# Rows on all partitions from columns: transposes of a broadcast column in place of products with a fixed matrix

## Chip, cores and metric

The kernel runs as one program on one core of a Trainium2 chip. The metric is the time of one execution in device microseconds (us). The engines are called as in the profile: PE (TensorE, matrix products), PEld (its weight loads), DVE (VectorE), ACT (ScalarE), POOL (GpSimd), and SP, whose queue issues the DMAs.

## What is computed

The reference takes 256 tokens of width 1024 in f32 through two networks, one behind the other. The first has two layers, each with a feed-forward block, a mixer and a second feed-forward block; the mixer is a hybrid (a state-space scan, "SSD", beside an mLSTM) in layer 0 and a sparse attention in layer 1. The second has two layers, each with three branches (gated MLP, retention, gated delta rule), gates and an output product. The parts that the change touches, cut short:

```python
# feed-forward block, before: x + 0.5 * swiglu(rms_norm(x))
y = xf * rsqrt(mean(xf * xf) + EPS) * g
# hybrid, SSD: decays between the tokens t and s of one chunk of 128
acs = cumsum(dt * A)
Lm = exp(where(t >= s, acs[t] - acs[s], -inf))
# hybrid, mLSTM: stabilised weights
Dm = where(t >= s, bcs[t] - bcs[s] + li[s], -inf)
m_t = maximum(max(Dm, axis=s), bcs + m_in)
S = (q @ k.T) * exp(Dm - m_t)
# delta rule, per direction, chunks of 64
gc = cumsum(g)
decay = exp(where(i >= j, gc[i] - gc[j], -inf))
lower = where(i > j, ((k * b) @ k.T) * decay, 0)
u, w = solve_triangular(lower + eye, rhs)
```

All four need the same thing at one point: a value per token, which lies in a column (token t on partition t), is wanted as a row that every partition holds (element t of the row belongs to token t), so that differences such as `acs[t] - acs[s]` can be formed on a 128 x 128 tile.

## The kernel before, in words

**Tiling.** The tokens are two tiles of 128. Each weight matrix comes from memory once, in units of 128 x 2048 f32, by DMAs from SP's queue (L273; three buffers). Every unit is split in halves of 1024 columns. ACT makes a rounded copy `hi` of a half (L218), DVE the rest `lo` = raw - `hi` in two instructions of 512 columns (L222), and there are four buffers each for `hi` and `lo`. An f32 product of the weights is then three products of this split form (L306 to L308, `mm3`): hi*hi, hi*lo and lo*hi. Activations are turned for these products by transposes against the identity matrix (`flip`, L478).

**Small products in plain f32.** Beside these large products there are small ones in plain f32, among them the ones that the change touches. They use a fixed trick: with a column v broadcast along the free dimension as the stationary operand, and a fixed matrix M as the moving one, the product holds on every partition the row v^T M. With M the identity (`ident`) this is the row of v itself; with M the triangular matrix `tri` (ones where the column index is at least the row index; `rtri` for the reverse direction) it is the running sum of v as a row.

**The four places.**

- Feed-forward block (`ffn`, L499; four calls). `rstd[t]`, the reciprocal root of a token's mean square, is spread to a row by two products with `ident` (L519), copied by ACT, and used from the second group of columns on, to scale the gate.
- Hybrid, decays (`decays`, L722; called for two groups of 8 heads). One product with `tri` sums all columns `a` to running sums (L668), which L670 copies to `cs`. Per group, chunk and head the product at L730 makes the running sum as a row once more, out of `a` and `tri`: 2 x 2 x 8 = 32 products into four-head tiles of PSUM. L733 on DVE subtracts the column `cs` and cuts off with `cap`; exponentials and products follow.
- Hybrid, mLSTM. Running maxima are formed on 4 partitions (one per head) as rows `R`; L811 negates two of them (`nR`, 4 x 256); four transposes (L814) turn `R` into columns `pw`; L816 and the exponentials make weights `w` from them. Behind a turn of side work, L828 spreads the rows of `nR` over all partitions: four products, each of a column of `ident[:4]` broadcast to 4 x 128 with `nR`, 256 columns. L832 on DVE takes them up.
- Delta rule (`delta`, L1293; once in each of the second network's two layers). Four products sum the columns `gs` to running sums (L1356 to L1359), which L1361 copies to `gc` on DVE. Then for two directions, two tiles and four heads L1368 makes the running sums as rows out of `gs` and `tri` or `rtri`: 16 products. L1372 on DVE and L1375 and L1376 on ACT make the decays `D`; products of keys with keys (L1390) and L1394 and L1398 on DVE fill the triangular system `U`, and L1405 adds the two directions. From there DMAs (L1424, L1428) carry it to the layout in which POOL solves 32 x 32 blocks (L1430 to L1436), and DMAs bring it back (L1443 to L1446). Later the blocks are put together; this stage begins with L1487 and the transposes at L1412.

**What sets the order.** In the hybrid and in the second network two generators are woven: a chain of dependent small steps, and side work (large weight products of other branches). The tables FILL (L602) and SIDE (L1245) say how many steps of side work follow each step of the chain. On top of this the instructions' order on each engine is set by the framework's planner when the program is built: it simulates all engines with durations of its own and takes the next ready instruction by priority, which is the order of writing. In sections marked `manual` (the sparse attention, the start and the ends of the down products) the written order stays. None of the four places lies in such a section.

Of the kernel before, what the change touches and what calls it, by code (L numbers as in the profile page):

```python
# [13 lines left out]
OP = mybir.AluOpType  # L14
# [32 lines left out]
class Entry:  # L47
# [17 lines left out]
    def load(self, dram, between=None):  # L65
        self.raw.append(self.net.fetch(dram, 2048, between))
# [53 lines left out]
class Net:  # L120
# [43 lines left out]
    def dram(self, shape):  # L164
        self.n += 1
        return self.dp.tile(shape, F32, name=f"dram{self.n}")

    def load_const(self, name, cols, parts=128):
        t = self.const(cols, parts=parts)
        self.nc.sync.dma_start(t, self.ins[name])  # L170
        return t
# [327 lines left out]
    def ffn(self, f, then):  # L499

        nc = self.nc
        V, A, PE = nc.vector, nc.scalar, nc.tensor
        hT, rstd, ps = self.entry.hT, self.entry.rstd, self.entry.out
        hid = Wide(self.f, 0)

        hid.grow(self.f)
        p = self.pt().rearrange("p (t j c) -> p t j c", j=2, t=2)
        for t in range(2):
            sg, hd = self.t2(256), self.t2(256)
            A.activation(sg, ps[t][:, :256], AF.Silu, scale=rstd[t])  # L510
            V.tensor_tensor(hd, ps[t][:, 256:], sg, OP.mult)
            for j in range(2):
                PE.transpose(p[:, t, j, :], hd[:, j * 128:(j + 1) * 128], self.ident)
        parts = lambda j: (a[:, :, j % 4:j % 4 + 2, :] for a in hid.half[-1])
        self.split(*parts(0), p)

        pr = self.pt()
        for t in range(2):
            PE.matmul(pr[:, t * 128:(t + 1) * 128], rstd[t].to_broadcast([128, 128]), self.ident, start=True, stop=True)  # L519
        row = self.l2(256)  # L520
        A.activation(row, pr[:, :256], AF.Copy)
        half = [self.small(1) for _ in range(2)]
        for t in range(2):
            nc.gpsimd.tensor_scalar(half[t], rstd[t], 0.5, None, op0=OP.mult)

        for j in range(2, 2 * NFG):
            if j % 4 == 0:
                hid.grow(self.f if j < 16 else self.g)
            if j % 2 == 0:
                hd = self.t2().rearrange("p (t j c) -> p t j c", t=2, j=2)  # L530
            gate, up = (x[:, :256] for x in self.group_w(self.ins["wgw"][f, j - 2], hT))
            sg = self.t2(256)
            V.tensor_tensor(sg, gate, row, OP.mult)
            A.activation(sg, sg, AF.Silu)
            tc = lambda z: z.rearrange("p (t c) -> p t c", t=2)
            V.tensor_tensor(hd[:, :, j % 2, :], tc(up), tc(sg), OP.mult)
            if j % 2:
                self.split(*parts(j - 1), hd)

        def done(t, cb, p):  # L540
            s = self.x[t][:, cb * 512:(cb + 1) * 512]
            V.scalar_tensor_tensor(s, p, half[t], s, op0=OP.mult, op1=OP.add)  # L542

        self.down(self.ins["wdn"][f], 2 * NFG, hid.tok, done, then)
# [60 lines left out]
class Hybrid:  # L605
    def hybrid(self, then):
        nc = self.nc
        ins = self.ins
        V, A, PE, G = nc.vector, nc.scalar, nc.tensor, nc.gpsimd
        mm = PE.matmul  # L610
# [36 lines left out]
        def chain():  # L647
# [16 lines left out]
            a = self.small(40).rearrange("p (t c) -> p t c", t=2)  # L664
# [4 lines left out]
            cs = self.small(40).rearrange("p (t c) -> p t c", t=2)  # L669
# [52 lines left out]
            def decays(g):  # L722

                for c in range(2):
                    seg[c] = self.g().rearrange("p (e t) -> p e t", e=8)
                    for hb in range(2):
                        pr = self.pt().rearrange("p (e t) -> p e t", e=4)
                        for e in range(4):
                            h = g * 8 + hb * 4 + e
                            mm(pr[:, e, :], a[:, c, h:h + 1].to_broadcast([128, 128]), self.tri, start=True, stop=True)  # L730
                        for e in range(4):
                            h = g * 8 + hb * 4 + e
                            V.scalar_tensor_tensor(seg[c][:, hb * 4 + e, :], pr[:, e, :], cs[:, c, h:h + 1], self.cap,  # L733
                                                   op0=OP.subtract, op1=OP.min)
                for c in range(2):
                    for hb in range(2):
                        half = seg[c][:, hb * 4:hb * 4 + 4]
                        A.activation(half, half, AF.Exp)
                        V.tensor_tensor(half, half, cb[:, c, g, None, :].to_broadcast([128, 4, 128]), OP.mult)
# [39 lines left out]
            A.activation(bt, pb[:, :256].rearrange("p (g n) -> p g n", g=2), AF.Copy)  # L779
            states(0)  # L780
            decays(0)
            yield next(fill)
            inputs(1)
            outputs(0)
            yield next(fill)
            turn(0)
            states(1)
            decays(1)
            yield next(fill)
            outputs(1)  # L790
# [10 lines left out]
            R = self.t2()  # L801
# [5 lines left out]
            V.tensor_tensor_scan(r4[:, 1], u4[:, 1], u4[:, 1], m1[:4], OP.max, OP.max)  # L807
            V.tensor_scalar(r4[:, 2], r4[:, 1], -1.0, m1[:4], op0=OP.mult, op1=OP.add)
            V.tensor_scalar(r4[:, 3], u4[:, 0], r4[:, 0, 127:128], None, op0=OP.subtract)
            nR = self.t2(256)  # L810
            V.tensor_scalar(nR[:4], R[:4, :256], -1.0, None, op0=OP.mult)  # L811
            pw = self.pt()
            for k in range(4):
                PE.transpose(pw[:, k * 4:k * 4 + 4], r4[:, k], self.ident[:4, :4])  # L814
# [2 lines left out]
                            pw[:, :8].rearrange("p (t c) -> p t c", t=2), OP.add)  # L817
            A.activation(w[:, :8], w[:, :8], AF.Exp, scale=-1.0)
            A.activation(w[:, 8:], pw[:, 8:16], AF.Exp)
            em = w[:, :8].rearrange("p (t c) -> p t c", t=2)  # L820
            yield next(fill)
            turn(1)
# [2 lines left out]
            for hb in range(2):  # L825
                pr = self.pt().rearrange("p (h c s) -> p h c s", h=2, c=2)
                for h in range(2):
                    mm(pr[:, h].rearrange("p c s -> p (c s)"),  # L828
                       self.ident[:4, 2 * hb + h:2 * hb + h + 1].to_broadcast([4, 128]), nR[:4], start=True, stop=True)
                for h in range(2):  # L830
                    for c in range(2):
                        V.scalar_tensor_tensor(P[c][:, 2 * hb + h, :], pr[:, h, c, :], u[:, c, 2 * hb + h:2 * hb + h + 1],  # L832
                                               self.cap, op0=OP.add, op1=OP.min)
# [15 lines left out]
            for h in range(4):  # L849
                p = self.pt()  # L850
# [4 lines left out]
            for c in range(2):  # L855
                for h in range(4):
                    p = self.pt()
# [390 lines left out]
class Second:  # L1248
# [29 lines left out]
    def second(self, l, then, end=None):  # L1278
        nc, ins = self.nc, self.ins
        V, A, PE, G = nc.vector, nc.scalar, nc.tensor, nc.gpsimd  # L1280
        mm = PE.matmul
# [11 lines left out]
        def delta(y_c):  # L1293
# [17 lines left out]
            gs = self.small(16)  # L1311
# [48 lines left out]
            gc = self.small(24)  # L1360
# [3 lines left out]
            for d, t in order:  # L1364
                pr = v4(self.pt())
                for h in range(4):
                    c = d * 8 + t * 4 + h
                    mm(pr[:, h, :], gs[:, c:c + 1].to_broadcast([128, 128]), self.rtri if d else self.tri,  # L1368
                       start=True, stop=True)
                for h in range(4):  # L1370
                    c = d * 8 + t * 4 + h
                    V.scalar_tensor_tensor(D[d][:, t, h, :], pr[:, h, :], gc[:, c:c + 1], self.rcap if d else self.cap,  # L1372
                                           op0=OP.subtract, op1=OP.min)
                    if t != d:
                        A.activation(Dc[d][:, h, :], pr[:, h, :], AF.Exp, bias=gc[:, 16 + d * 4 + h:17 + d * 4 + h])  # L1375
                A.activation(D[d][:, t], D[d][:, t], AF.Exp)  # L1376
# [54 lines left out]
            for e in range(31):  # L1431
                n, m, cs = 31 - e, e // 2 + 1, slice(e + 1, 32)
                a = flat(Y[1])[:, :m * n].rearrange("p (q i) -> p q i", i=n)
# [23 lines left out]
            for gr in range(2):  # L1457
                ps = self.group_w(ww[4 + gr], hT)
                for j in range(2):
                    acc = conv(8 + 2 * gr + j, ps[j][:, :256])  # L1460
                    for t in range(2):
                        c = (2 * gr + j) * 128
# [21 lines left out]
            for t in range(2):  # L1484
                for d in range(2):
                    c = C[2 * d].rearrange("p (t h c) -> p t h c", t=2, h=4)[:, t, :, None].to_broadcast([128, 4, 4, 32])
                    (G if d else V).tensor_tensor(r4(Y[d][:, t]), r4(bc4(self.near)), c, OP.mult)  # L1487
            for lev in range(2):
                flip()
                T1 = []  # L1490
                for t in range(2):
                    p = v4(self.pt())
# [5 lines left out]
                for t in range(2):  # L1498
                    p = v4(self.pt())
                    for h in range(4):  # L1500
                        mm(p[:, h, :], T1[t][:, h, :], Y[1][:, t, h, :], start=True, stop=True)
                    a, b, keep = Y[0][:, t], Y[1][:, t], T1[t]
# [8 lines left out]
            for i in range(3):  # L1511
                for d in range(2):
                    a, b = (1, 0) if d else (0, 1)
                    p = v4(self.pt())
                    for h in range(4):
                        if i == 1:
                            mm(p[:, h, :], Uc[d][:, h, :], W[d][:, a, h, :], start=True, stop=True)
                        else:
                            mm(p[:, h, :], Y[d][:, b if i else a, h, :], (r1[d] if i else vp[a])[:, h, :],
                               start=True, stop=True)  # L1520
# [6 lines left out]
            for t in range(2):  # L1527
                po = v4(self.pt())
                d = 1 - t
# [13 lines left out]
                for h in range(4):  # L1543
                    V.scalar_tensor_tensor(v4(yo)[:, h, :], po[:, h, :], f[:, h:h + 1], v4(zd[t])[:, h, :],
                                           op0=OP.mult, op1=OP.mult)
# [156 lines left out]
        done = []  # L1702
        y_c = Wide(None, 0)
        self.weave(delta(y_c), others(y_c), done)

        mT = Wide(self.g, 2)
        out = self.down_steps(ins["bout"][l], 8, mT.tok, self.add_x if then else self.finish(end), then)
# [195 lines left out]
```

## Time and profile before

| | us |
|---|---|
| three runs | 1704.15, 1702.5, 1704.07 |
| their median | 1704.07 |
| the profiled execution's own time | 1703.21 |
| its span in the profile | 1701.4 |

The mean granted clock of PE in the profiled execution was 0.994 of full speed.

How to read the lines of the profile that follow: a line of the page such as `PE 1682.9 (99%) x10518` gives busy time in us, its share of the span and the number of instructions. A line of waits such as `ACT hi L218 <- PE mm L308: 242.9, 139, 5.9` says that ACT's instructions at L218 waited 242.9 us in total for PE's at L308, 139 times, at most 5.9. In a group by form, `275/275/275, 27.0 to 916.5` are minimum, median and maximum duration in ns, and the starts of the first and the last in us. A line of the timeline begins with start and length in us of a run of like instructions on one engine; a bracket at its end holds how long the engine sat idle before it and for what. A line of the windows has the stretch, its length, then busy us (and instructions) of PE, PEld, DVE, ACT and POOL, then the granted clock, the share of time in which the DMA engines were busy, and GB/s.

Names of tiles: `hi`, `lo`, `raw` are the weights and their split forms, `tr` and `mm` the two kinds of PSUM tile, `sm` a small SBUF tile, `c` a constant, `g`, `f`, `l` and `t` larger SBUF tiles.

### The profile page before, as it was taken

The page shows a single profiled execution, that of the slowest core. Times are in us where ns is not written, and L with a number is a line of the kernel's source. Part 1 is how long each engine was busy: PE and PEld are TensorE (multiplying, and loading weights), DVE is VectorE, ACT ScalarE, POOL GpSimd, SP SyncE. Part 2 cuts the span into 40 slices and gives each one's busy share as a digit, 9 for nine tenths or more (in the row PEclk, how much of TensorE's full clock was granted, in tenths as well). Part 3 has the DMA queues.
Part 4 walks back from the last instruction along what each step waited for, and adds up shares of the span by engine and source line. Part 5 has one row for each costly group of instructions (what it writes and reads, how often), then busy time and mean ns, then how long its engine had stood idle before and what let it go on. Part 6 is the DMA issues. An engine that isn't in the chain of part 4 may idle for free.

```text
span 1701.4 us, 27046 instructions
## 1 busy us (share of the span) xinstructions
PE 1682.9 (99%) x10518; PEld 1493.3 (88%) x10518; DVE 1129.1 (66%) x2220; ACT 889.4 (52%) x1324; POOL 284.8 (17%) x448
## 2 busy tenths in 40 slices
PE   9999999999999999999999999999999999999998
PEld 8998799788999899988789998788898878889886
DVE  7665588665665466647956665567785776778476
ACT  7444476465444354434565444476446347644643
POOL 3000021001000010000111000143632204364211
PEclk9999999999999999999899999999999999999999
DMA  8555454344555555554234556455444445554442
GB/s 276 192 180 210 152 176 147 127 158 150 208 189 189 195 174 197 179 206 161 82 104 160 196 177 226 150 185 167 157 149 149 167 163 198 153 181 149 138 151 95
DMA packets 63296, 287.65 MB, mean 169 GB/s; under 512 B 23744, under 2 KB 26688, under 8 KB 30144
## 3 DMA queue, kind: packets, MB, share of 16 engines
q1 hardware_dynamic: 63168, 285.92, 48.5%
q8 instruction: 83, 1.36, 0.3%
q14 instruction: 45, 0.37, 0.1%
HBM read 283.28 MB, written 2.62 MB: 168 GB/s over the span
## 4 chain that ended last, share of the span: by engine, by line
PE 89%; DVE 3%; POOL 3%; ACT 2%; DMA 1%; issue 1%; SPq 0%; POOLq 0%; ACTq 0%; DVEq 0%
PE mm L306 26%; PE mm L308 26%; PE mm L307 26%; PE tr L478 1%; POOL g L1436 1%; POOL g L1434 1%; DVE lo L222 1%; PE tr L1194 1%; PE tr L1041 1%; PE tr L1390 1%; DVE g L85 1%; PE mm L1155 0%; DMA dram<-g 0%; POOL sm L232 0%; PE tr L1368 0%
## 5 line engine op out<-in xcount | busy, mean ns | idle before, releaser
L222 DVE TENSOR_TENSOR lo<-raw,hi 128x512 fp32r<-128x512 f32 x996 | 665.1, 712 | 421.6 <-ACT hi L218 417.1
L218 ACT ACTIVATE hi<-raw 128x1024 fp32r<-128x1024 f32 (+1 forms) x502 | 524.7, 1050 | 554.0 <-PE mm L308 242.9
L307 PE MATMUL mm<-g,hi 128*128 128x256 f32 x1760 | 493.9, 281 | 0.0
L306 PE MATMUL mm<-g,hi 128*128 128x256 f32 x1760 | 493.8, 281 | 0.0
L308 PE MATMUL mm<-g,lo 128*128 128x256 f32 x1760 | 492.2, 281 | 0.0
L306 PEld LDWEIGHTS mm<-g,hi 128*128 128x128 f32 x1760 | 331.0, 188 | 1.0 <-issue 0.2
L307 PEld LDWEIGHTS mm<-g,hi 128*128 128x128 f32 x1760 | 331.2, 188 | 0.6
L308 PEld LDWEIGHTS mm<-g,lo 128*128 128x128 f32 x1760 | 330.0, 188 | 0.2 <-issue 0.2
L306 PE MATMUL mm<-hi,g 128*128 128x512 f32 (+1 forms) x784 | 312.2, 399 | 0.7 <-ACT g L218 0.7
L307 PE MATMUL mm<-lo,g 128*128 128x512 f32 (+1 forms) x784 | 309.9, 396 | 0.3
L308 PE MATMUL mm<-hi,g 128*128 128x512 f32 (+1 forms) x784 | 308.8, 395 | 1.0 <-DVE g L491 1.0
L308 PEld LDWEIGHTS mm<-hi,g 128*128 128x128 f32 x784 | 147.4, 188 | 34.8 <-DVE g L491 1.9
L307 PEld LDWEIGHTS mm<-lo,g 128*128 128x128 f32 x784 | 147.8, 189 | 32.9 <-DVE lo L222 1.9
L306 PEld LDWEIGHTS mm<-hi,g 128*128 128x128 f32 x784 | 147.9, 189 | 32.6 <-ACT g L218 1.2
L307 PE MATMUL mm<-lo,f 128*128 128x512 f32 x416 | 163.8, 394 | 0.0
L308 PE MATMUL mm<-hi,f 128*128 128x512 f32 x416 | 163.7, 396 | 0.0
L306 PE MATMUL mm<-hi,f 128*128 128x512 f32 x416 | 162.3, 401 | 0.9 <-ACT f L1558 0.9
L229 POOL TENSOR_SCALAR sm<-sm 128x1 f32<-128x1 f32 x18 | 7.8, 434 | 574.7 <-ACT c L70 573.9
L306 PEld LDWEIGHTS mm<-hi,f 128*128 128x128 f32 x416 | 78.1, 188 | 20.4 <-ACT f L1558 1.8
L308 PEld LDWEIGHTS mm<-hi,f 128*128 128x128 f32 x416 | 78.1, 188 | 19.0
L307 PEld LDWEIGHTS mm<-lo,f 128*128 128x128 f32 x416 | 78.2, 188 | 17.9
L90 POOL TENSOR_TENSOR g<-x,g 128x512 f32<-128x512 f32 x12 | 15.4, 1296 | 237.9 <-DVE x L542 174.0
(410 smaller groups left out, 1704.4 us busy)
## 6 DMA issues: line engine op xcount, KB each, us to landing
raw<-in_wgw_dram SPq DMA_DIRECT2D x80, 1024.0 KB, 4.9
raw<-in_wdn_dram SPq DMA_DIRECT2D x44, 1024.0 KB, 4.8
raw<-in_bx_dram SPq DMA_DIRECT2D x24, 1024.0 KB, 4.8
raw<-in_bgate_dram SPq DMA_DIRECT2D x24, 1024.0 KB, 4.8
raw<-in_bw_dram SPq DMA_DIRECT2D x20, 1024.0 KB, 5.0
raw<-in_hyx_dram SPq DMA_DIRECT2D x12, 1024.0 KB, 4.9
raw<-in_bproj_dram SPq DMA_DIRECT2D x12, 1024.0 KB, 4.8
raw<-in_hyw_dram SPq DMA_DIRECT2D x10, 1024.0 KB, 4.9
```

The lines of the kernel that those rows point to most:

```text
L85: self.nc.vector.scalar_tensor_tensor(self.src[t][:, s], self.net.x[t][:, s], self.rstd[t], self.gain[:, s], op0=OP.mult, op1=OP.mult)
L218: nc.scalar.activation(hi, src, AF.Copy)
L222: (nc.gpsimd if o and help else nc.vector).tensor_tensor(lo[..., s], src[..., s], hi[..., s].bitcast(F32), OP.subtract)
L306: mm(out, a[0], b[0], start=start, stop=False)
L307: mm(out, a[0], b[1], start=False, stop=False)
L308: mm(out, a[1], b[0], start=False, stop=stop)
L478: self.nc.tensor.transpose(p[:, k, :], src[:, k * 128:(k + 1) * 128], self.ident)
L1041: PE.transpose(p[:, j * 128:(j + 1) * 128], src[:, j * 128:(j + 1) * 128], self.ident)
L1194: mm(po[:, 2 * (j0 + i) + r, :], P[n][:, i, c, :], v[:, c, :], start=c == 0, stop=c == t)
L1390: mm(p[:, jt, :], k[h][:, jt * 128:(jt + 1) * 128], right[h], start=True, stop=True)
L1434: G.tensor_tensor(a, Z[:, :m, e:e + 1].to_broadcast([128, m, n]), B[:, e:e + 1, cs].to_broadcast([128, m, n]), OP.mult)
L1436: G.tensor_tensor(Z[:, :m, cs], Z[:, :m, cs], a, OP.add)
```

## The change

A new function `spread` transposes the broadcast column against `ident` in place of a product. A transpose of a tile whose 128 columns are all the same column gives a tile whose 128 rows are all the same row. Feed-forward: the same column, spread by transposes. Decays: the running sum `cs` is spread, in place of a product of `a` with `tri`. Delta: `gc` is spread, in place of products of `gs` with `tri` and `rtri`. mLSTM: `nR` becomes a small tile of 128 x 8, made from the transposed columns `pw` after the exponentials, and eight transposes of 128 columns take the place of four products of 256; the negation of 4 x 256 at L811 goes.

```diff
+    def spread(self, out, col):
+
+        self.nc.tensor.transpose(out, col.to_broadcast([128, 128]), self.ident)
 ...
         pr = self.pt()
         for t in range(2):
-            PE.matmul(pr[:, t * 128:(t + 1) * 128], rstd[t].to_broadcast([128, 128]), self.ident, start=True, stop=True)
+            self.spread(pr[:, t * 128:(t + 1) * 128], rstd[t])
 ...
                         for e in range(4):
                             h = g * 8 + hb * 4 + e
-                            mm(pr[:, e, :], a[:, c, h:h + 1].to_broadcast([128, 128]), self.tri, start=True, stop=True)
+                            self.spread(pr[:, e, :], cs[:, c, h:h + 1])
 ...
-            nR = self.t2(256)
-            V.tensor_scalar(nR[:4], R[:4, :256], -1.0, None, op0=OP.mult)
             pw = self.pt()
             for k in range(4):
                 PE.transpose(pw[:, k * 4:k * 4 + 4], r4[:, k], self.ident[:4, :4])
 ...
             A.activation(w[:, 8:], pw[:, 8:16], AF.Exp)
+            nR = self.small(8)
+            V.tensor_scalar(nR, pw[:, :8], -1.0, None, op0=OP.mult)
 ...
                 for h in range(2):
-                    mm(pr[:, h].rearrange("p c s -> p (c s)"),
-                       self.ident[:4, 2 * hb + h:2 * hb + h + 1].to_broadcast([4, 128]), nR[:4], start=True, stop=True)
+                    for c in range(2):
+                        self.spread(pr[:, h, c], nR[:, 4 * c + 2 * hb + h:4 * c + 2 * hb + h + 1])
 ...
                 for h in range(4):
                     c = d * 8 + t * 4 + h
-                    mm(pr[:, h, :], gs[:, c:c + 1].to_broadcast([128, 128]), self.rtri if d else self.tri,
-                       start=True, stop=True)
+                    self.spread(pr[:, h, :], gc[:, c:c + 1])
```

## The prediction

> **What bounds the kernel now.** I read the page first (busy times, the chain that ended last), then the waits, then one by one the lines that the diff touches, then timelines around them.
>
> ```profile
> PE 1682.9 (99%) x10518; PEld 1493.3 (88%) x10518; DVE 1129.1 (66%) x2220; ACT 889.4 (52%) x1324; POOL 284.8 (17%) x448
> ...
> PE 89%; DVE 3%; POOL 3%; ACT 2%; DMA 1%; issue 1%; SPq 0%; POOLq 0%; ACTq 0%; DVEq 0%
> ```
>
> PE is busy 99% of the span and holds 89% of the chain. Busy PE need not be PE at its peak, so the next question is who waits for whom.
>
> ```profile
> ACT hi L218 <- PE mm L308: 242.9, 139, 5.9
> ...
> ACT hi L218 <- PE mm L307: 142.4, 95, 6.1
> ```
>
> ```profile
> PE tr L478 <- DVE g L85: 2.1, 4, 0.5
> ...
> PE tr L1412 <- DVE g L1487: 0.6, 1, 0.6
> ```
>
> The split of the weights on ScalarE (L218) waits 385 us in total for PE, most of it for buffers that PE has not yet given back. PE's longest waits in total are 2 us and less. So in nearly all stages a microsecond less of PE work is a microsecond less of time. The last of these rows is the exception that matters here: in the first of the two delta layers PE waits at L1412 for a chain that runs through GpSimd.
>
> **The price of one product and of one transpose.**
>
> ```profile
> L519 PE MATMUL tr<-c,sm x16: 275/275/275, 27.0 to 916.5; 128*128 128x128 f32 x16
> L730 PE MATMUL tr<-c,sm x64: 270/275/275, 252.8 to 296.9; 128*128 128x128 f32 x64
> L1368 PE MATMUL tr<-c,sm x64: 275/275/356, 1142.6 to 1448.6; 128*128 128x128 f32 x64
> L1412 PE MATMUL tr<-c,g x32: 270/272/300, 1231.1 to 1551.9; 128*128 128x128 f32 x32
> ```
>
> The code issues 8 products at L519 (four FFNs, two each), 32 at L730 and 32 at L1368 (two layers of 16). Each line has twice as many records: a plain f32 product runs through the array twice. L1412 is an existing transpose; the code issues 2 layers x 2 levels x 8 = 32, and there are 32 records, so a transpose of f32 runs once. The durations (275 and 272 ns) overlap; what counts is the distance between starts.
>
> ```profile
> 252.75 2.84 PE L730 MATMUL tr<-c,sm 128*128 128x128 f32 x24
> 382.02 1.03 PE L478 MATMUL tr<-c,t 128*128 128x128 f32 x8
> 1142.57 3.82 PE L1368 MATMUL tr<-c,sm 128*128 128x128 f32 x32
> 1146.15 0.48 PE L306 MATMUL mm<-hi,g 128*128 128x512 f32 x1
> ```
>
> 24 records of L730 take 2.84 us with the last one's 0.275 at the end: 2.565 / 23 = 0.1115 us apart, so 0.223 us a product. Eight transposes take 1.03: (1.03 - 0.272) / 7 = 0.108 us each. Replacing a product by a transpose saves 0.115 us of PE. [...]
>
> **The change part by part.**
>
> FFN: 8 products become 8 transposes of the same column: 8 x 0.115 = 0.92 us. No new wait, the column is `rstd` as before.
>
> Decays of the hybrid: 32 x 0.115 = 3.68 us. The column is now the running sum `cs`, copied to SBUF at L670:
>
> ```profile
> 237.09 0.19 DVE L670 COPY sm<-tr 128x40 f32<-128x40 f32 x1
> ```
>
> That is 15 us before the first L730 (252.75), so nothing waits.
>
> mLSTM: four products of 4 rows by 256 columns become eight transposes; a DVE instruction (L811) goes and a small one on the transposed rows comes.
>
> ```profile
> 332.55 0.77 PE L478 MATMUL tr<-c,t 128*128 128x128 f32 x5
> 332.66 0.16 DVE L816 TENSOR_TENSOR sm<-sm,tr 128x8 f32<-128x8 f32 x1 [0.81 <-PE tr L814]
> ```
>
> The next two rows are of the chain that ended last (start, us, what):
>
> ```profile
> 333.32 1.05 PE tr L828 x4
> ...
> 338.52 1.06 PE tr L828 x4
> ```
>
> Each of these rows is two products in two passes; they hold PE for 1.05 + 1.06 = 2.11 us. Eight transposes take 8 x 0.108 = 0.86. Saved 1.25. The new column comes from the same PSUM tile as L816, one instruction of about 0.16 us behind it: ready at 332.66 + 0.16 + 0.16 = 332.98. Five transposes of the flip (L478) keep PE until 333.3, so I cost this new wait at nothing; without that cover it would be some 0.3 us, once.
>
> Delta, two layers: 2 x 16 x 0.115 = 3.68 us. Here the change adds a wait. The products read `gs`; the transposes read `gc`, which DVE copies (L1361) out of PSUM after the four products just ahead.
>
> ```profile
> 1140.27 1.29 DVE L222 TENSOR_TENSOR lo<-raw,hi 128x512 fp32r<-128x512 f32 x2 [1.48 <-ACT hi L218]
> 1142.35 0.36 PE L1359 MATMUL tr<-sm,c 128*128 128x4 f32 x2
> 1142.75 0.18 DVE L1361 COPY sm<-tr 128x24 f32<-128x24 f32 x1 [1.19 <-PE tr L1359]
> ```
>
> Before, L1368 started at 1142.57. After, it can't start before 1142.75 + 0.18 = 1142.93 and a weight load behind it: up to 0.55 us of idle PE per layer if nothing fills it. Queued behind the waiting transposes on PE are the weight products of the side work. One half of their weights has been split since 1141.6 (the L222 row), and the first of them ran at 1146.15, so the planner can put two of them into the gap, and the cost is then zero. Bounds 0 and 0.55; I take 0.25 for the second layer. In the first layer something larger decides:
>
> ```profile
> 1157.64 1.29 DVE L222 TENSOR_TENSOR lo<-raw,hi 128x512 fp32r<-128x512 f32 x2 [0.59 <-ACT hi L218]
> 1162.73 1.22 DVE L1405 TENSOR_TENSOR g<-g,g 128x1024 f32<-128x1024 f32 x1
> 1173.49 2.14 POOL L1430 COPY g<-g 64x1024 f32<-64x1024 f32 x1 [27.47 <-DMA g<-dram]
> 1232.47 0.63 PE L1412 MATMUL tr<-c,g 128*128 128x128 f32 x4 [0.56 <-DVE g L1487]
> 1530.71 2.39 DVE L1487 TENSOR_TENSOR g<-c,g 128x512 f32<-128x512 f32 x2
> 1534.51 0.60 PE L1412 MATMUL tr<-c,g 128*128 128x128 f32 x4
> ```
>
> From L1405 the triangular solve goes by DMA to GpSimd and back, and PE meets it at L1412. In the first layer PE already waits there, so a PE that comes sooner only waits longer, unless the solve starts sooner too. Its start hangs on DVE, which from L1372 to L1405 has hardly a gap (third time in these rows of the windows; second row the sum over 1140 to 1165):
>
> ```profile
> 1160.00:1165.00 5.00, 5.00 (x32) 4.38 (x31) 5.00 (x15) 2.14 (x3) 0.00 (x0) 1.00 0.25 103
> sum 25.00, PE 25.00 PEld 21.67 DVE 21.17 ACT 16.32 POOL 3.70; mean PE 5.00 PEld 4.33 DVE 4.23 ACT 3.26 POOL 0.74
> ```
>
> The one gap that I take PE's lead to close is the 0.59 us ahead of 1157.64, where the split waits for ScalarE, which waits for a buffer from PE. So of 1.84 us in this layer I keep 0.59: minus 1.25. In the second layer L1487 is through at 1530.71 + 2.39 = 1533.10 and L1412's second run starts at 1534.51: 1.4 us of room, and 0.59 more by the same gap, which holds the 1.84.
>
> Sum: 0.92 + 3.68 + 1.25 + 3.68 = 9.53, minus 1.25, minus 0.25 = 8.0 us. The profiled execution took 1703.21 us (its span 1701.4 and 1.8 outside, which stays): 1695.2. The median of the runs, 1704.07, is 0.86 above it: 1696.1. A measurement of this kernel can tell about 0.2%, 3.4 us, from no change: faster is below 1700.7, slower above 1707.5.
>
> **The rivals.**
>
> *VectorE takes the lead back.* In the first group of decays DVE is full:
>
> ```profile
> 255.00:260.00 5.00, 5.00 (x45) 5.00 (x44) 5.00 (x16) 3.48 (x5) 0.00 (x0) 1.00 0.46 188
> 253.85 3.19 DVE L733 SCALAR_TENSOR_TENSOR g<-tr,sm,c 128x128 f32<-128x128 f32 x12 [0.46 <-PE tr L730]
> ```
>
> (Busy PE, PEld, DVE, ACT, POOL in the first row.) If the split weights were used as soon as they are made, PE could only gain what DVE gains: the 0.46 us that DVE waits for the first product in this group, taken for the second group too, and 0.59 in each delta layer. With FFN and mLSTM: 0.92 + 1.18 + 0.92 + 1.25 = 4.27, so 1699.8, near the edge of what can be told. For it: DVE's full stretch. Against it: the 385 us in which the split waits for PE, so the weights lie ready ahead.
>
> *The solve is put back.* The planner that orders each engine sees PE idle for `gc` and runs side products first, and the transposes, L1372 and with them the solve come later. Products of the weights follow each other every 0.23 us:
>
> ```profile
> 1140.38 0.39 PE L306 MATMUL mm<-hi,g 128*128 128x512 f32 x1
> 1140.60 0.39 PE L307 MATMUL mm<-lo,g 128*128 128x512 f32 x1
> ```
>
> A half (1024 columns: two blocks of 512, two tiles of rows, three products each) is 12 of them, 2.8 us. If two halves go first, the solve starts 5.6 us later in both layers; PE then waits at L1412 for 5.6 us in the first and 5.6 - 1.4 = 4.2 in the second, 9.8 in all against 0.92 + 3.68 + 1.25 = 5.85 saved elsewhere: 4.0 us slower, 1708.1. With a delay of d the two waits are 2d - 1.4, so it ends slower than before from d = 3.6 us on, and measurably so from about 5.3. For it: no room at L1412 in layer one. Against: the copy L1361 waits for nobody but PE (its row), and the gap is 0.4 us, not 5.
>
> *A broadcast column isn't transposed at 0.108.* No row shows a transpose of a zero-step column. The nearest dear row is that of the first ten transposes of the run:
>
> ```profile
> 1.39 2.40 PE L556 MATMUL tr<-c 128*128 128x128 f32 x10 [1.39 <-DVE c L178]
> 876.00:884.00 8.00, 8.00 (x47) 6.08 (x46) 4.03 (x16) 6.20 (x16) 0.00 (x0) 1.00 0.00 0
> ```
>
> With the last one's duration taken as 0.275, (2.40 - 0.275) / 9 = 0.236 us each. At that price the 72 transposes lose 72 x 0.013 = 0.94 and mLSTM gains 2.11 - 8 x 0.236 = 0.22: 0.7 slower, 1704.8, the same. The sum turns below zero from 0.227 on. The same would come if runs of transposes cost PE its clock. [...] The trace does not bear it out: 876 to 884, a stretch of attention with transposes throughout, has a granted clock of 1.00 (third figure from the end).
>
> **How the numbers follow.** Forecast 0.68, VectorE 0.17, the solve put back 0.08, transposes dear 0.07. Predicted 1696.1. The low end keeps all 9.53 (1694.5) with half a microsecond for the spread of the runs: 1694.0. The high end takes in the forecast with both waits of `gc` unfilled, another 0.85, and a plan worse by two microseconds, and the VectorE case with its own spread: 1702.0; left out are the last two rivals, 0.15. Faster: nearly all of the forecast (0.66) and half of the VectorE case: 0.75. Same: the other half, the dear transposes, a little of the forecast: 0.16. Slower 0.09.
>
> **What would show it.** Right: the four lines have one record per call, 0.108 us apart; L1368's 16 take 1.7 us in place of 3.6; PE's idle time at L1412 in layer one grows to about 1.8 us and in layer two stays near nothing; PE's wait for L1361 is under 0.6 us. Wrong: L730 followed by a wait of PE for L222 (VectorE), L1405 later in the span than its 1162.73 of now, less what PE has gained by then (solve put back), starts 0.22 us apart or a clock below 1.00 in these stretches (dear transposes).

## The result, and the profile after

The changed kernel is slower: 1720.26 us (median of 4 runs, 1718.51 to 1723.64) against 1703.74 of before (median of 4, 1702.5 to 1704.15). The ratio is 1.010, with a 95% interval of 1.0089 to 1.0112. The forecast was 1696.1. The profiled execution took 1723.64 us, the longest of the four; its span is 1721.8. One of the five executions of a later kernel, wait_no_transpose, took 3653.85 us, about twice as long as all others, and is left out of its figures.

Busy times and the chain that ended last, from the page of the kernel after:

```profile
PE 1685.5 (98%) x10446; PEld 1493.7 (87%) x10446; DVE 1128.8 (66%) x2220; ACT 898.2 (52%) x1332; POOL 287.3 (17%) x448
...
PE 83%; POOL 5%; DVE 4%; DMA 3%; ACT 2%; issue 2%; SPq 1%; POOLq 0%; ACTq 0%; DVEq 0%
```

PE has 72 instructions fewer, as meant, but its share of the chain fell from 89% to 83%, and POOL and the DMAs took up what it lost. ACT has 8 instructions more. The new helper `spread` and the shorter delta line move the line numbers: what was L306 is L310, L1361 is L1365, L1372 is L1375, L1405 is L1408, L1412 is L1415, and all spread rows are L170. PE's waits:

```profile
PE tr L1415 <- DVE g L1490: 14.4, 4, 7.8
...
PE tr L1393 <- ACT l L1378: 1.6, 2, 0.8
```

The wait at the place where PE meets the solve was 0.6 us before and is 14.4 now, in both layers.

**Where the time went.** I took the starts of all instructions of DVE, ACT and POOL that both kernels have in equal number, and the median of their differences (after less before) by stage. The changed kernel is 2.7 us late ahead of the first changed instruction (an offset of its start, which lies between 0.1 and 2.7 us in the executions profiled here). Then: 2.4 behind the first feed-forward rows, -1.2 behind the decays, -2.9 behind the mLSTM and ahead of the delta rule still -2.0. Behind the first delta layer it is +8.5, behind the second +20.1. So the first three parts gained 4.7 of the 5.85 us forecast for them, and the delta layers lost 10.5 and 11.6 us.

The price of a transpose is right. By form, the groups of L170, then its first run of twelve in the timeline:

```profile
L170 PE MATMUL tr<-c,sm x80: 270/272/273, 29.7 to 1460.0; 128*128 128x128 f32 x80
```

```profile
255.17 1.47 PE L170 MATMUL tr<-c,sm 128*128 128x128 f32 x12
```

80 calls are 80 records, and (1.47 - 0.272) / 11 = 0.109 us apart.

**The delta rule, first layer.** The timeline of after from the sums to the solve's input:

```profile
1140.37 0.36 PE L1363 MATMUL tr<-sm,c 128*128 128x4 f32 x2
1140.77 0.18 DVE L1365 COPY sm<-tr 128x24 f32<-128x24 f32 x1 [1.18 <-PE tr L1363]
1145.30 1.91 PE L170 MATMUL tr<-c,sm 128*128 128x128 f32 x16
...
1172.63 1.20 DVE L1408 TENSOR_TENSOR g<-g,g 128x1024 f32<-128x1024 f32 x1
```

`gc` is ready at 1140.95, but the rows start at 1145.30: PE's program has 20 side products (L310 to L312) between the sums and the rows. PE doesn't wait there, it works on something else for 4.5 us. From the copy to U0 + U1 it was 1162.73 - 1142.75 = 19.98 us before and is 1172.63 - 1140.77 = 31.86 now. So 4.35 us of late rows became 11.9 of late solve. ScalarE shows a part of how (timeline of ACT):

```profile
1153.67 0.63 ACT L1378 ACTIVATE l<-tr,sm 128x128 f32<-128x128 f32 x2 [1.11 <-DVE g L1375]
1154.32 1.28 ACT L1561 ACT_TABLE_LOAD   x1
1155.61 0.60 ACT L1561 ACTIVATE f<-mm 128x512 f32<-128x512 f32 x1
1156.23 1.28 ACT L1378 ACT_TABLE_LOAD   x1
1157.52 0.37 ACT L1378 ACTIVATE l<-tr,sm 128x128 f32<-128x128 f32 x1
1157.79 0.62 ACT L1379 ACTIVATE g<-g 128x512 f32<-128x512 f32 x1
1158.43 1.28 ACT L1561 ACT_TABLE_LOAD   x1
1159.72 0.60 ACT L1561 ACTIVATE f<-mm 128x512 f32<-128x512 f32 x1
...
1161.28 1.28 ACT L1378 ACT_TABLE_LOAD   x1
1162.58 0.37 ACT L1378 ACTIVATE l<-tr,sm 128x128 f32<-128x128 f32 x1
```

The side products that went ahead are those of a gate. Their sigmoids (L1561) now fall due between the exponentials of the decays (L1378, L1379), and each of the four changes from one function to the other in these rows comes with a table load of 1.28 us. The span has 55 such loads, before it had 47; three of the new ones lie in each delta layer. In these rows the activation starts 0.01 us behind the load.

VectorE, which forms the solve's input, waits for these exponentials and for the weights that ScalarE splits (timeline of DVE):

```profile
1158.44 0.61 DVE L1397 SCALAR_TENSOR_TENSOR g<-g,sm,tr 128x128 f32<-128x128 f32 x2 [2.99 <-ACT g L1379]
1161.29 1.29 DVE L226 TENSOR_TENSOR lo<-raw,hi 128x512 fp32r<-128x512 f32 x2 [2.25 <-ACT hi L222]
1163.49 0.61 DVE L1397 SCALAR_TENSOR_TENSOR g<-g,sm,tr 128x128 f32<-128x128 f32 x2 [0.91 <-ACT g L1379]
```

From the copy to U0 + U1 DVE idles 9.2 us in all, before it was 2.4: 6.8 of the 11.9. The rest is side work that went ahead on DVE as well: 14 instructions of the split (L226) lie in this stretch in place of 8, 3.7 us, and eight of another branch (L1622) in place of three, 1.3 us.

At the far end the wait also takes PE's clock. The wait of PE, and windows of 4 us around it (the first figure after the length is busy PE, the third from the end the granted clock):

```profile
1237.37 1.12 PE L1415 MATMUL tr<-c,g 128*128 128x128 f32 x4 [7.80 <-DVE g L1490]
```

```profile
1228.00:1232.00 4.00, 1.57 (x14) 1.36 (x12) 0.00 (x0) 0.00 (x0) 0.00 (x0) 1.00 0.92 221
1232.00:1236.00 4.00, 0.00 (x0) 0.00 (x0) 0.20 (x1) 1.01 (x3) 0.00 (x0) 0.60 0.64 170
1236.00:1240.00 4.00, 2.40 (x11) 2.14 (x11) 3.96 (x5) 2.50 (x4) 3.12 (x2) 0.50 0.32 125
1240.00:1244.00 4.00, 4.00 (x25) 4.00 (x24) 4.00 (x8) 1.14 (x2) 0.14 (x1) 0.62 0.33 98
1244.00:1248.00 4.00, 4.00 (x37) 4.00 (x36) 2.62 (x6) 2.08 (x3) 3.27 (x4) 1.00 1.00 412
```

PE stops at 1229.57; the second row (0.60 on average over 4 us: 1.00 for 0.8 and 0.50 for 3.2) has the clock fall to 0.50 at 1232.8, 3.2 us later, and by the fourth it comes back at about 1243, 5.7 us behind the restart. The busy time at the lower clock costs 2.40 x 0.50 + 4.00 x 0.38 = 2.7 us. The layer adds up: 8.0 of PE's waits for L1490, 1.4 of two smaller ones, less the 0.6 of before, plus 2.7, less 1.84 saved on the rows, is 9.7; measured 10.5. In the second layer the same waits come to 8.3 us (6.4, 1.1 and 0.8), and the clock is at 0.50 twice, from 1499.0 to 1502.4 and from 1546.8 to 1557.1, which costs 4.6 us reckoned in the same way. Less 1.84 that is 11.1; measured 11.6.

### The profile page after: what moved, and what is told of

It is laid out like the page before. It is cut to its first block, busy times and chain, and to the rows that moved or that the text cites. A ratio compares the mean times of both kernels' runs of the same rounds, so it can differ in the third digit from the quotient of the medians.

```text
span 1721.8 us, 26916 instructions
## 1 busy us (share of the span) xinstructions
PE 1685.5 (98%) x10446; PEld 1493.7 (87%) x10446; DVE 1128.8 (66%) x2220; ACT 898.2 (52%) x1332; POOL 287.3 (17%) x448
## 4 chain that ended last, share of the span: by engine, by line
PE 83%; POOL 5%; DVE 4%; DMA 3%; ACT 2%; issue 2%; SPq 1%; POOLq 0%; ACTq 0%; DVEq 0%
PE mm L310 25%; PE mm L311 25%; PE mm L312 25%; POOL g L1439 2%; POOL g L1437 2%; DMA dram<-g 1%; DVE lo L226 1%; PE tr L482 1%; DMA g<-dram 1%; PE tr L1198 1%; PE tr L1045 1%; POOL sm L236 1%; ACT hi L222 1%; PE tr L170 1%; DVE g L85 1%
## 5 line engine op out<-in xcount | busy, mean ns | idle before, releaser
L226 DVE TENSOR_TENSOR lo<-raw,hi 128x512 fp32r<-128x512 f32 x996 | 666.7, 713 | 412.4 <-ACT hi L222 410.8
L310 PE MATMUL mm<-g,hi 128*128 128x256 f32 x1760 | 496.4, 283 | 0.0
L312 PE MATMUL mm<-g,lo 128*128 128x256 f32 x1760 | 494.0, 282 | 0.0
L310 PEld LDWEIGHTS mm<-g,hi 128*128 128x128 f32 x1760 | 332.5, 189 | 1.3 <-issue 0.2
L312 PEld LDWEIGHTS mm<-g,lo 128*128 128x128 f32 x1760 | 332.4, 189 | 0.2 <-issue 0.2
L310 PE MATMUL mm<-hi,g 128*128 128x512 f32 (+1 forms) x784 | 313.0, 400 | 0.7 <-ACT g L222 0.7
L312 PE MATMUL mm<-hi,g 128*128 128x512 f32 (+1 forms) x784 | 309.7, 396 | 0.3 <-DVE g L495 0.3
L312 PEld LDWEIGHTS mm<-hi,g 128*128 128x128 f32 x784 | 148.1, 189 | 34.0 <-DVE g L495 1.2
L310 PEld LDWEIGHTS mm<-hi,g 128*128 128x128 f32 x784 | 148.5, 189 | 32.3 <-ACT g L222 1.2
L312 PE MATMUL mm<-hi,f 128*128 128x512 f32 x416 | 163.9, 397 | 1.6 <-DVE f L226 1.6
L310 PE MATMUL mm<-hi,f 128*128 128x512 f32 x416 | 162.8, 402 | 0.9 <-ACT f L1561 0.9
L312 PEld LDWEIGHTS mm<-hi,f 128*128 128x128 f32 x416 | 78.5, 189 | 21.2 <-DVE f L226 2.5
L310 PEld LDWEIGHTS mm<-hi,f 128*128 128x128 f32 x416 | 78.5, 189 | 21.1 <-ACT f L1561 1.8
```

What stands on the lines that cost most here:

```text
L226: (nc.gpsimd if o and help else nc.vector).tensor_tensor(lo[..., s], src[..., s], hi[..., s].bitcast(F32), OP.subtract)
L310: mm(out, a[0], b[0], start=start, stop=False)
L312: mm(out, a[1], b[0], start=False, stop=stop)
```

## The experiments

Theory A: the transposes wait for `gc`, the planner therefore puts side products ahead of them, and the late solve makes PE wait. Theory B: transposes are dear or take PE's clock. Theory C: any edit shuffles the plan by this much. All ratios are to runs of the kernel before on the same chip.

**delta_back** undoes the delta part alone.

```diff
-                    self.spread(pr[:, h, :], gc[:, c:c + 1])
+                    mm(pr[:, h, :], gs[:, c:c + 1].to_broadcast([128, 128]), self.rtri if d else self.tri,
+                       start=True, stop=True)
```

> The changed kernel with one part undone: the delta rule's rows come from products of gs with tri and rtri again; the other three parts stay changed. Theory A (the delta rows wait for gc, the planner puts 20 side products ahead of them, the solve starts some 10 us later in each layer and PE waits for it): all of the loss is gone and the gains of the other three parts are left, 0.92 + 3.68 + 1.25 = 5.85, so 1703.7 - 5.9 = 1697.9 (0.9966 of before), and U0 + U1 of the first delta layer comes about 4 us sooner than before. Theory B (runs of transposes cost PE its clock or are dear): 40 of 72 + 8 transposes remain, so about half of the 16.5 us remains: 1710 to 1712. Theory C (any edit reshuffles the plan by such amounts): still 1712 to 1721.

Measured: 1698.69 us, before 1703.6, ratio 0.997 (0.9959 to 0.9982). All of the loss is gone, and 4.9 of the 5.85 us of the other parts are there; by the interval it is between 3.1 and 7.0. U0 + U1 comes at 1158.77, 4.0 us sooner than before, as theory A asked. Theory C falls, and theory B for the 40 transposes that stay. For the 32 of the delta rule the next two runs decide.

**rows_first** keeps the whole change and adds an order on PE: the first side product written after the delta rows is issued behind them.

```diff
+        first = mm(out, a[0], b[0], start=start, stop=False)
+        if self.hold is not None:
+            self.tc.add_manual_dep(first.ins, self.hold, mybir.DependencyInfo(
+                mybir.DependencyClass.NoSync, mybir.DependencyReason.DATA), reason="hold")
+            self.hold = None
 ...
-                    self.spread(pr[:, h, :], gc[:, c:c + 1])
+                    last = self.spread(pr[:, h, :], gc[:, c:c + 1])
 ...
+            self.hold = last.ins.name
```

> The changed kernel, with an edge of order (no wait) that puts the first side product written after the delta rows behind them on PE. gc is made where the change makes it, so PE really waits for it on the chip, but nothing is put ahead of the rows. Theory A: the wait itself is 0.4 to 0.55 us per layer, and the loss was the order: 1703.7 - 9.5 + 1.1 + 0.6 to 1.25 for the solve of layer one, 1695.5 to 1696.5. Rival to A (the wait for gc itself is long, or PE's stall takes its clock): 1705 to 1720. Theory B: 1720.

Measured: 1697.33, ratio 0.9964 (0.9951 to 0.9978), faster than both kernels. Its rows in the timeline, and its wait for the solve:

```profile
1137.10 1.96 PE L170 MATMUL tr<-c,sm 128*128 128x128 f32 x16 [0.28 <-DVE sm L1371]
```

```profile
PE tr L1422 <- DVE g L1497: 1.6, 2, 0.8
```

The wait for `gc` itself costs 0.28 us a layer. The loss was the order: all 32 transposes of the delta rule are still there, so theory B falls for them too. The time is 0.8 us above theory A's range, less than the interval can tell. In the trace PE waits 0.8 us for the solve in both layers, not in the first alone, since from the copy to U0 + U1 it takes 22.27 us here against 19.98 before. The 2.3 us are side work on DVE: ten instructions of the split in place of eight (1.2 us) and seven of the other branch (L1629 here) in place of three (1.0 us); DVE idles 2.4 us as before. The intervals of delta_back and rows_first overlap for the most part, so whether the delta part gains anything with its rows in place is not shown.

**wait_no_transpose** has the wait without transposes in the delta rule.

```diff
-                    self.spread(pr[:, h, :], gc[:, c:c + 1])
+                    mm(pr[:, h, :], gc[:, c:c + 1].to_broadcast([128, 128]), self.ident, start=True, stop=True)
```

> The changed kernel, but the delta rows are products of the broadcast column gc with the identity: the same wait for gc, no transposes there. Theory A: as slow as the changed kernel, since the wait and the order are the same, plus up to 3.7 us for the dearer rows as far as PE's wait for the solve does not hide them: 1720 to 1724. Theory B: only the 32 transposes of the delta rule cost; without them the loss is gone or halved: 1698 to 1712.

Measured: 1709.46, ratio 1.0035 (1.0022 to 1.0049): slower than before, but not as slow as the changed kernel. That is a miss for theory A (1720 to 1724) and lies in theory B's range, though B has fallen by rows_first. The 20 side products stand ahead of the rows as in the changed kernel:

```profile
1137.52 0.36 PE L1363 MATMUL tr<-sm,c 128*128 128x4 f32 x2
1142.46 3.73 PE L1372 MATMUL tr<-c,sm 128*128 128x128 f32 x32
```

But the span has 49 table loads and not 55. So the order does put the solve back without any transpose in the delta rule, and theory A lacked a second step: the alternating functions on ACT. The next run takes that step away with the transposes in place.

**sigmoid_behind** leaves the rows late and orders the next sigmoid behind the last exponential.

```diff
-                A.activation(D[d][:, t], D[d][:, t], AF.Exp)
+                exp = A.activation(D[d][:, t], D[d][:, t], AF.Exp)
 ...
+            self.exp = exp.ins.name
 ...
-                A.activation(sig[t][:, cb * 512:(cb + 1) * 512], p, AF.Sigmoid)
+                z = A.activation(sig[t][:, cb * 512:(cb + 1) * 512], p, AF.Sigmoid)
+                if self.exp is not None:
+                    self.tc.add_manual_dep(z.ins, self.exp, mybir.DependencyInfo(
+                        mybir.DependencyClass.NoSync, mybir.DependencyReason.DATA), reason="behind")
+                    self.exp = None
```

> The changed kernel (rows of the delta rule still 20 side products late), with an edge of order that puts the next sigmoid of the side work behind the last exponential of the decays on ScalarE, so that the two functions no longer alternate there. Theory A, in two steps (the late rows let the side work's sigmoid fall due between the exponentials, and each change of function costs a table load of 1.28 us on ScalarE): 49 table loads in place of 55, U0 + U1 some 5 us earlier against the sums than the 32 us of the changed kernel, time 1705 to 1710. Rival (the 4.5 us by which the rows are late do it all, the table loads lie beside it): 1717 to 1721.

Measured: 1710.47, ratio 1.0032 (1.002 to 1.0045), 0.5 us above the range of theory A and far from the rival. The same stretch of ACT:

```profile
1153.92 0.35 ACT L1380 ACTIVATE l<-tr,sm 128x128 f32<-128x128 f32 x1
1154.17 0.63 ACT L1381 ACTIVATE g<-g 128x512 f32<-128x512 f32 x1
1154.82 1.28 ACT L1564 ACT_TABLE_LOAD   x1
1156.11 1.09 ACT L1564 ACTIVATE f<-mm 128x512 f32<-128x512 f32 x2
```

One load in place of four in this stretch, 49 in all. From the copy to U0 + U1 it takes 26.99 us, 4.9 less than in the changed kernel: DVE idles 5.3 us in this stretch in place of 9.2, which is 3.8 less, as much as three loads, and four of the eight instructions of L1622 (another line number here) no longer come first (1.0 us). By the ratios, 1.0100 against 1.0032, the alternating functions cost 0.0068 x 1704 = 11.6 us of the loss, with what hangs on them further down (PE's waits and its clock).

**rows_behind_12** is rows_first, except that 12 side products may go ahead (the order begins at the fifth triple written after the rows).

```diff
-        if self.hold is not None:
+        self.count += 1
+        if self.hold is not None and self.count > 4:
 ...
-            self.hold = None
+            if self.count == 12:
+                self.hold = None
 ...
-            self.hold = last.ins.name
+            self.hold, self.count = last.ins.name, 0
```

> As rows_first, but 12 side products are let ahead of the delta rows, in place of none there and 20 in the changed kernel; the table loads stay at 49. Theory A (each product ahead puts the solve back by 0.23 us, and PE, which waits 0.8 us for the solve already in rows_first, pays it in full): 2.5 to 2.8 us a layer, and up to 1.5 for a lower clock after the longer wait: 1702.3 to 1705.9. Rival (a delay costs nothing until the functions alternate on ScalarE): 1697 to 1699.

Measured: 1711.38, ratio 1.0034 (1.0021 to 1.0046). The direction is theory A's, the size was not: against rows_first it is 0.0070 x 1704 = 12 us for 2.8 us of products in two layers. The wait grew from 0.8 to 4.5 in the first layer, and with it came the clock:

```profile
PE tr L1424 <- DVE g L1499: 8.4, 4, 4.5
```

```profile
1228.00:1230.00 2.00, 1.77 (x8) 1.51 (x9) 2.00 (x2) 0.50 (x2) 2.00 (x2) 0.50 0.00 0
1230.00:1232.00 2.00, 2.00 (x11) 2.00 (x10) 2.00 (x3) 1.70 (x3) 0.69 (x1) 0.50 0.00 0
1232.00:1234.00 2.00, 2.00 (x11) 2.00 (x10) 2.00 (x4) 0.00 (x0) 0.00 (x0) 0.50 0.56 94
```

(1.77 + 2.00 + 2.00) x 0.50 = 2.9 us in this layer, about as much again in the other, where I had allowed 1.5. From the copy to U0 + U1 it takes 3.5 us more than in rows_first, and PE's waits for the solve grow by as much a layer, 6.8 in all; with some 6 of clock that makes up the 12. So the delay is paid in full, as theory A says, but it is 3.5 us for 2.8 us of products, and the clock is twice as dear as allowed. (The profiled execution, 1707.8, is the shortest of this kernel's five.) The wait of 4.5 us here cost 2.9 us of clock, that of 7.8 in the changed kernel 2.7, and those of 0.8 in rows_first none (its granted clock over these stretches is 1.00).

**delta_only** puts the delta part alone into the kernel before (`spread` and its one line, as in the change).

> The kernel before with the delta part of the change alone. Theory A (all of the loss is in the two delta layers, whatever the other parts do): 10.5 and 11.7 us lost there by the traces, 1703.7 + 21 to 22.5 = 1724.7 to 1726.2. Theory C (the parts disturb each other's plan): clearly less, 1704 to 1718.

Measured: 1727.88, before 1704.67, ratio 1.0135 (1.0121 to 1.0148): 23.2 us slower, where theory A asked for 21 to 22.5. PE's waits:

```profile
PE tr L1415 <- DVE g L1490: 17.3, 4, 8.7
```

The loss is in this part, and it is larger here since the others do not pay some of it back: the changed kernel's 16.5 us and delta_back's 4.9 make 21.4, which the intervals cannot tell from 23.2. So nothing shows that the parts disturb each other's plan.

**gc_early** makes `gc` sooner: the four sums and the copy are written ahead of the keys.

```diff
+            pc = self.pt()
+            mm(pc[:, 0:8], self.tri, gs[:, 0:8], start=True, stop=True)
 ...
+            V.tensor_copy(gc, pc[:, :24])
             k = yield from keys(0, ss[:, :8])
             yield SIDE[0]
-            pc = self.pt()
-            mm(pc[:, 0:8], self.tri, gs[:, 0:8], start=True, stop=True)
 ...
-            V.tensor_copy(gc, pc[:, :24])
```

> The changed kernel with all transposes, but the four products of the running sums and the copy to gc are written ahead of the keys of the delta rule, some 60 PE instructions earlier, so that gc lies ready when the rows are due. Theory A: no wait, the rows stand right where they stood before and the solve starts as early as before or 2 us sooner; forecast 8.0 to 9.5 us under before: 1694.2 to 1695.7. Theory B: as slow as the changed kernel, 1720. Theory C: 1712 to 1721.

Measured: 1706.57, ratio 1.0019 (1.001 to 1.0028). A miss: better than the change, yet no gain. The sums have a wait of their own at the new place:

```profile
PE tr L1357 <- POOL sm L1317: 4.4, 2, 2.2
```

GpSimd hasn't finished `gs` there, and PE stands still for 2.2 us in each layer. I had looked at who needs `gc` and not at what `gc` needs. Behind each of the two waits the clock is low as well:

```profile
1127.80:1131.00 3.20, 3.20 (x9) 2.42 (x9) 0.00 (x0) 0.60 (x1) 0.00 (x0) 0.50 0.08 31
1431.50:1438.20 6.70, 6.70 (x24) 6.02 (x25) 0.55 (x2) 2.12 (x3) 0.00 (x0) 0.50 0.36 146
```

That is (3.20 + 6.70) x 0.50 = 5.0 us, more than the 4.4 of the waits. With 1.4 more of PE's wait for the solve (2.0 in place of 0.6) it makes 10.8 of the 11 to 12.5 us that are missing from the forecast.

The runs side by side; "ahead" is the number of side products between the sums and the rows, "to U0 + U1" the time from the copy of `gc` in the first layer, "wait" PE's total wait for the solve:

| kernel | ahead | to U0 + U1 | table loads | wait | ratio |
|---|---|---|---|---|---|
| before | 0 | 19.98 | 47 | 0.6 | 1 |
| rows_first | 0 | 22.27 | 49 | 1.6 | 0.9964 |
| rows_behind_12 | 12 | 25.81 | 49 | 8.4 | 1.0034 |
| wait_no_transpose | 20 | 26.08 | 49 | 6.3 | 1.0035 |
| sigmoid_behind | 20 | 26.99 | 49 | 11.2 | 1.0032 |
| after | 20 | 31.86 | 55 | 14.4 | 1.0100 |
| delta_only | 20 | 31.89 | 53 | 17.3 | 1.0135 |

The ratios of rows_behind_12, wait_no_transpose and sigmoid_behind can't be told apart, their intervals overlap almost wholly; so the time does not follow the waits alone (in wait_no_transpose the rows are dearer by 1.84 us a layer, and PE waits less behind them). Two of the loads come with the other parts of the change (delta_back has 49 as well), so the delta part brings six, in delta_only as in the changed kernel.

## Why the prediction was wrong

**Right:** that PE's work bounds nearly all stages, the price of a transpose (0.108, measured 0.109), the sum of feed-forward, decays and mLSTM (5.85 forecast; delta_back measured 4.9, with 3.1 to 7.0 as its interval), the mLSTM's new wait at nothing (no wait of L170 for DVE in that stage), and the bounds of the wait for `gc` (0 to 0.55, 0.25 taken; 0.28 measured in rows_first, where nothing goes ahead). Runs of transposes did not take PE's clock here: over the two runs of 16 between other products in the changed kernel (1145.00 to 1148.00 and 1458.00 to 1460.30) it was 1.00. The row that the prediction brought against such a loss was weaker than it says: from 876 to 884 PE runs three groups of 4 to 8 transposes (L1041) among products, not transposes throughout.

**The step that failed** is the sentence on what fills the gap: "so the planner can put two of them into the gap, and the cost is then zero". It took the chip's times for the planner's. On the chip `gc` is there 0.2 us behind the last sum's end; the plan, made with the planner's own picture, had 20 products in a place for two. So the new wait wasn't free filling but a change of order, fixed when the program was built. In the sum, the delta part (3.68 minus 1.25 for the solve minus 0.25 for this wait) was to gain 2.2 us; the two delta layers lost 10.5 and 11.6.

**The rival that came true** was the solve put back, at a chance of 0.08. What spoke against it ("the gap is 0.4 us, not 5") failed for the same reason. Its price failed as well: for the 4.35 us by which the rows were late it gave waits of 2 x 4.35 - 1.4 = 7.3 us, against 5.85 saved elsewhere, 1.5 us slower; measured 16.5. It counted each late microsecond once. The chain behind the rows carried it further in three ways: table loads on ACT, since the side work that went ahead brought sigmoids with it (11.6 us of the time, by sigmoid_behind); side work that went ahead on DVE too (5.0 us of the solve's delay in the first layer); and the half clock around the waits (2.7 us in the first layer, 4.6 in the second). The condition set in the prediction, L1405 later in the span, is what the profile shows: 1172.63 against 1162.73.

**Still open:** why the planner takes `gc` for ready only some 20 products later. No trace shows its picture; that the copy stands behind splits of weights on DVE in its reckoning is a guess that wasn't tried.

## What to carry to other kernels

Where a planner fixes the order, a new dependency is priced by what the plan puts into the gap, not by the wait that the chip would show; pin the order of the step that feeds a long chain, then the wait itself is small (0.28 us here in place of a delay of 4.35). Before saving work on the bounding engine, look for the place where it meets a chain of other engines without slack: there a late start was paid in full in this case, and again in what it brought along (three more loads of function tables on ScalarE in each delta layer, 1.28 us each; 5.0 us of side work on VectorE in the first; 2.7 and 4.6 us of PE's clock). The same look is due where a step is moved up: ask what it needs itself, as gc_early shows.

## What the runs showed of the hardware

- PE's clock fell to 0.50 around several of its waits and stayed there for some time behind them. In the changed kernel's first delta layer it fell to 0.50 3.2 us after PE had stopped and came back 5.7 us behind the restart; in the second layer it fell 2.0 us after the stop and came back 6.1 us behind the restart. Delta layers in which PE idled for 2.9 to 9 us for the solve lost 1.4 to 3.1 us to the clock, the waits of 2.2 us in gc_early 1.6 and 3.4, those of 0.8 us in rows_first none. The length of the wait alone did not tell here: behind one of 1.07 us in the changed kernel's second layer the clock was at 0.50 for 3.4 us, behind one of 2.19 us near the start of its span (ended at 8.10) it stayed at 1.00.
- Alternating between exponential and sigmoid on ACT came with one load of 1.28 us at each of the four changes in the changed kernel's first delta layer, and with one at the single change of that stretch in sigmoid_behind.
- A plain f32 transpose of a column broadcast with zero step took 0.109 us here, as much as one of a full tile (0.108) and half of a plain f32 product (0.223).
